# Eight heads' attention weights transposed by the DMA engines, and a written order for the last heads' steps

## The chip, the cores and the metric

The kernel runs on one core of a Trainium2 chip. The metric is the time of one execution on the device in microseconds (us), given as the median of a few runs. The engines are TensorE (PE, with its weight loads shown as PEld), VectorE (DVE), ScalarE (ACT), GpSimd (POOL) and SyncE (SP), which issues the DMAs; each works through its own queue of instructions in order and waits on semaphores for the others.

## The reference

One decoder layer on 256 tokens of width 1024, in float32. With SEQ equal to MOBA_BLOCK there is one key block, so the block selection falls away and the attention is plain causal attention with 8 heads of 128.

```python
def reference(x, attn_norm, attn_w_qkv, attn_w_o, ..., ffn_norm, ffn_w_in, ffn_w_out, final_norm):
    x = x + moba_attention(rms_norm(x, attn_norm[0]), attn_w_qkv[0], attn_w_o[0])
    x = x + swiglu(rms_norm(x, ffn_norm[0]), ffn_w_in[0], ffn_w_out[0])
    return rms_norm(x, final_norm)
# moba_attention: p = softmax(mask(q k^T / sqrt(128))); out = concat(p v) w_o
# swiglu:         g, u = split(h w_in); silu(g) * u times w_out      (hidden width 2816)
```

## The kernel before

Every large product is made as three products of parts: a float32 matrix is split into a rounded part `hi` (a cast on ACT, L84) and the rest `lo` (a subtraction on DVE, L85), and `mm` (L102 to L105) adds hi·hi, hi·lo and lo·hi in PSUM. So each weight tile of 128 x 2048 that is loaded (`early`, L99) costs two casts on ACT and two subtractions on DVE of 128 x 1024 each.

The stages follow each other: the value projection (L192), for each of 8 heads the projection of q and k (`project`), then the output projection `wo` (L335 to L340 and L354 to L372), the hidden layer of the channel mixer (`hidden`, from L389) and its output.

The attention of a head is cut into steps which lag behind each other by `follow`: `scores(h)` makes q·k on TensorE, adds the mask (DVE, L253), takes the exponential (ACT, L258) and scales by the sums (DVE, L263), which leaves the weights `pn[h]`, 128 x 384 (three 128 x 128 blocks, since the upper block of a causal mask is empty). `attend(h)` needs them transposed. It writes a PSUM bank of the pool `ps_b`, which has two, and reads it out into `oh` (ACT, L306) and `ol` (DVE, L307), the operands of head h's part of the output projection.

The transpose is done in two ways. Heads 0 to 5 (`BY_DMA = 6`): `turn_p(h)` copies the float32 weights on ACT into two planes of 16-bit halves (L269, into `planes_p`, one buffer) and has SP issue one DMA transpose of the planes (L271, into `turned_p`, two buffers); `transpose_p(h)` joins the halves again on ACT (L280). Heads 6 and 7: `transpose_p(h)` makes three transposes on TensorE (L289) into PSUM and copies the last block out on ACT (L296). Both then make `p0h` (ACT, L293) and `p0l` (DVE, L294), which `attend(h)` takes.

The output projection of a head is 12 products of 128 x 512 (`wo_mm`, two token tiles t, two halves n, three each). Before, the code goes through heads 0 to 4 and, behind each of heads 1 to 4, calls `follow`, which does the steps that are still open; heads 5 to 7 follow with the residual sums: for each (t, n) the sum is added to x (L364), multiplied by the gain (L366, `xg`), squared for the norm (ACT, L367) and transposed by four transposes on TensorE (`turn_x1`, L349), whose result is cast (ACT, L351) and subtracted (DVE, L352) as operands `x1h` and `x1l` of the hidden layer.

The code is not the order on the engines: a scheduler orders each engine's instructions from the order of the code and its own estimates, and fixes it when the program is built. A copy written within `keep_in_program_order` stays where it is written. In what follows the order is that of the built program.

## Time and profile before

| | before |
|---|---|
| median of 3 runs | 294.16 us (291.99, 294.46, 294.16) |
| the profiled execution | 292.13 us, of which span of its instructions 290.3 us |
| PE busy | 282.2 us, 97% of the span, 1481 matmuls |
| PEld busy | 241.4 us, 83% |
| DVE busy | 210.4 us, 72% |
| ACT busy | 196.8 us, 68% |
| DMA | 59.91 MB, mean 206 GB/s |
| granted TensorE clock | 0.996 of full speed |
| chain that ended last | PE 94%, DMA 2%, DVE 1%, ACT 1% |

The span goes from the first to the last instruction. Matmuls are pipelined: one is printed with 0.39 us but the next starts 0.23 us later, so what a matmul costs is read from start to start. The output projection lies at 80.8 to 107.3 us of the span.

### The profile page before, as it was taken

The page shows a single profiled execution, that of the slowest core. Times are in us where ns is not written, and L with a number is a line of the kernel's source. Part 1 is how long each engine was busy: PE and PEld are TensorE (multiplying, and loading weights), DVE is VectorE, ACT ScalarE, POOL GpSimd, SP SyncE. Part 2 cuts the span into 40 slices and gives each one's busy share as a digit, 9 for nine tenths or more (in the row PEclk, how much of TensorE's full clock was granted, in tenths as well). Part 3 has the DMA queues.
Part 4 walks back from the last instruction along what each step waited for, and adds up shares of the span by engine and source line. Part 5 has one row for each costly group of instructions (what it writes and reads, how often), then busy time and mean ns, then how long its engine had stood idle before and what let it go on. Part 6 is the DMA issues. An engine that isn't in the chain of part 4 may idle for free.

```text
span 290.3 us, 3904 instructions
## 1 busy us (share of the span) xinstructions
PE 282.2 (97%) x1481; PEld 241.4 (83%) x1481; DVE 210.4 (72%) x328; ACT 196.8 (68%) x295; POOL 1.3 (0%) x8
## 2 busy tenths in 40 slices
PE   7899999999999999999999999999999999999992
PEld 4688999999988888888888888888888888888881
DVE  3757988877776489648468468468959689987784
ACT  3786878777985388739659659659649687544443
POOL 1000000000000000000000000000000000000000
PEclk9999999999999999999999999999999999999998
DMA  6999785985565406785765875766363737770003
GB/s 202 414 424 419 284 290 102 369 264 174 172 189 218 163 38 202 256 273 164 282 215 160 277 219 159 275 212 137 144 181 54 275 54 279 281 256 35 0 0 144
DMA packets 25507, 59.91 MB, mean 206 GB/s; under 512 B 17425, under 2 KB 17809, under 8 KB 19601
## 3 DMA queue, kind: packets, MB, share of 16 engines
q1 hardware_dynamic: 25200, 59.28, 60.8%
q10 hardware_dynamic: 288, 0.39, 0.4%
q8 instruction: 11, 0.18, 0.3%
q14 instruction: 8, 0.06, 0.1%
HBM read 54.56 MB, written 1.05 MB: 192 GB/s over the span
## 4 chain that ended last, share of the span: by engine, by line
PE 94%; DMA 2%; DVE 1%; ACT 1%; SPq 0%; issue 0%
PE pmm L105 24%; PE pmm L103 24%; PE pmm L104 24%; PE pmm L192 7%; PE pb L105 2%; PE pb L104 2%; PE pb L103 2%; PE pa L104 2%; PE pa L105 2%; PE pa L103 2%; DMA first<-in_xw 2%; PE pb L349 1%; PE pb L305 1%; PE pb L247 1%; DVE x_sb L567 1%; SPq L132 0%
## 5 line engine op out<-in xcount | busy, mean ns | idle before, releaser
L85 DVE TENSOR_TENSOR lo<-raw,hi 128x1024 fp32r<-128x1024 f32 x80 | 95.9, 1221 | 22.8 <-ACT hi L84 22.7
L84 ACT CAST hi<-raw 128x1024 fp32r<-128x1024 f32 x80 | 81.5, 1048 | 12.3 <-issue 5.6
L103 PE MATMUL pmm<-hi,xh 128*128 128x512 f32 x176 | 68.6, 390 | 0.0
L104 PE MATMUL pmm<-lo,xh 128*128 128x512 f32 x176 | 68.6, 390 | 0.0
L105 PE MATMUL pmm<-hi,xl 128*128 128x512 f32 x176 | 68.5, 389 | 0.0
L105 PEld LDWEIGHTS pmm<-hi,xl 128*128 128x128 f32 x176 | 33.0, 188 | 6.9
L104 PEld LDWEIGHTS pmm<-lo,xh 128*128 128x128 f32 x176 | 33.0, 188 | 6.8
L103 PEld LDWEIGHTS pmm<-hi,xh 128*128 128x128 f32 x176 | 33.0, 188 | 6.8
L404 ACT ACTIVATE sg<-pmm,r 128x256 f32<-128x256 f32 x22 | 10.5, 476 | 30.4 <-PE pmm L105 30.4
L103 PE MATMUL pmm<-hi,first 128*128 128x512 f32 x76 | 30.2, 397 | 0.0
L104 PE MATMUL pmm<-lo,first 128*128 128x512 f32 x76 | 29.7, 390 | 0.0
L103 PE MATMUL pmm<-xh,hi 128*128 128x256 f32 x96 | 27.1, 283 | 0.0
L105 PE MATMUL pmm<-xh,lo 128*128 128x256 f32 x96 | 27.1, 283 | 0.0
L104 PE MATMUL pmm<-xl,hi 128*128 128x256 f32 x96 | 27.1, 282 | 0.0
L478 ACT CAST hi<-raw 128x1024 fp32r<-128x1024 f32 (+1 forms) x15 | 17.6, 1191 | 8.7 <-PE pa L105 3.8
L479 DVE TENSOR_TENSOR lo<-raw,hi 128x1024 fp32r<-128x1024 f32 (+1 forms) x15 | 20.5, 1397 | 3.2 <-ACT hi L478 3.2
L405 DVE SCALAR_TENSOR_TENSOR hs<-pmm,r,sg 128x256 f32<-128x256 f32 x22 | 10.5, 482 | 14.9 <-ACT sg L404 14.9
L103 PEld LDWEIGHTS pmm<-xh,hi 128*128 128x128 f32 x96 | 18.4, 192 | 0.0
L105 PEld LDWEIGHTS pmm<-xh,lo 128*128 128x128 f32 x96 | 18.4, 191 | 0.0
L104 PEld LDWEIGHTS pmm<-xl,hi 128*128 128x128 f32 x96 | 18.4, 191 | 0.0
L103 PEld LDWEIGHTS pmm<-hi,first 128*128 128x128 f32 x76 | 14.3, 188 | 2.7
L104 PEld LDWEIGHTS pmm<-lo,first 128*128 128x128 f32 x76 | 14.3, 188 | 2.7
(156 smaller groups left out, 457.6 us busy)
## 6 DMA issues: line engine op xcount, KB each, us to landing
raw<-in_w_in SPq DMA_DIRECT2D x22, 1024.0 KB, 4.9
raw<-in_w_out SPq DMA_DIRECT2D x11, 1024.0 KB, 4.8
raw<-in_wqk SPq DMA_DIRECT2D x8, 1024.0 KB, 10.8
raw<-in_wo SPq DMA_DIRECT2D x4, 1024.0 KB, 7.7
first<-in_xw SPq DMA_DIRECT2D x3, 640.0 KB, 8.1
second<-in_xw SPq DMA_DIRECT2D x2, 640.0 KB, 11.8
x_sb<-in_x SPq DMA_DIRECT2D x1, 1024.0 KB, 11.1
g_bc<-in_g SPq DMA_DIRECT2D x2, 512.0 KB, 4.5
```

The costliest lines, as they stand in the source:

```text
L84: nc.scalar.copy(hi, raw)
L85: nc.vector.tensor_sub(lo, raw, hi.bitcast(F32))
L103: nc.tensor.matmul(o, lhsT=lh, rhs=rh, start=first, stop=False)
L104: nc.tensor.matmul(o, lhsT=lh, rhs=rl, start=False, stop=False)
L105: nc.tensor.matmul(o, lhsT=ll, rhs=rh, start=False, stop=last)
L192: nc.tensor.matmul(pv[t][a // 512][:, a % 512 : a % 512 + b - a], lhsT=l[:, k, t * P : (t + 1) * P], rhs=r[:, a:b],  start=k == 0 and a % ...
L247: nc.tensor.matmul(ps[:, :P], lhsT=f[:, :P], rhs=f[:, T : T + P], start=True, stop=True)
L305: nc.tensor.matmul(po[:, P:], lhsT=v1[:, hs], rhs=p1, start=False, stop=True)
L404: nc.scalar.activation(sg, pf[t][:, 0], AF.Silu, scale=r2[t])
L405: nc.vector.scalar_tensor_tensor(hs_[c][:, :, t], pf[t][:, 1].rearrange("p (j f) -> p j f", j=2), r2[t], sg.rearrange("p (j f) -> p j f", ...
L478: nc.scalar.copy(h[:, a:b], r[:, a:b])
L479: nc.vector.tensor_sub(l[:, a:b], r[:, a:b], h[:, a:b].bitcast(F32))
```

## The change

`BY_DMA` falls away: all eight heads take the way through the planes, the DMA transpose and the join, and `transpose_p` without its TensorE branch is now `join_p`. In place of the loop with `follow` behind heads 1 to 4, the steps of heads 4 to 7 are written out between the heads' products, with parts of heads 5 and 6 moved ahead.

```diff
-        def transpose_p(h):
-            pp = joined_p[h % 2]
-            if h < BY_DMA:
...
-            else:
-                p = ps_a.tile([P, 3 * P], F32, name="pa")
-                for i in range(3):
-                    nc.tensor.transpose(p[:, i * P : (i + 1) * P], pn[h][:, i * P : (i + 1) * P], ident)
-                p1 = pp[:, T:]
...
+        def join_p(h):
+
+            p = joined_p[h % 2]
+            tc.keep_in_program_order(
+                nc.scalar.copy(
+                    p.bitcast(U16).rearrange("p (n w) -> p n w", w=2),
+                    turned_p[h % 2].rearrange("p (w n) -> p n w", w=2),
+                )
             )
             p0h = a2.tile([P, T], F32R, name="p0h")
             p0l = a2.tile([P, T], F32R, name="p0l")
             nc.scalar.copy(p0h, p[:, :T])
             nc.vector.tensor_sub(p0l, p[:, :T], p0h.bitcast(F32))
-            if h >= BY_DMA:
-                nc.scalar.copy(p1, p[:, T:])
-            pt[h] = p0h, p0l, p1
+            pt[h] = p0h, p0l, p[:, T:]
...
-                if step is scores and 0 <= i < BY_DMA:
+                if step is scores and 0 <= i < H:
                     turn_p(i)
...
-        for h in range(5):
+        def wo_head(h):
             for t in range(NT):
                 for n in range(2):
                     wo_mm(h, t, n)
-            if h:
-                follow(H + h - 1)
+
+
+        wo_head(0)
+        attend(4)
+        scores(7)
+        turn_p(7)
+        wo_head(1)
+        join_p(6)
+        attend(5)
+        wo_head(2)
+        wo_head(3)
+        join_p(7)
+        attend(6)
+        wo_head(4)
+        for h, t in ((5, 0), (6, 0)):
+            for n in range(2):
+                wo_mm(h, t, n)
+        attend(7)
+        for n in range(2):
+            wo_mm(5, 1, n)
...
-                if t == 0:
-                    for h, m in ((5, 0), (6, 0), (5, 1), (6, 1), (7, 0)) if n == 0 else ((7, 1),):
-                        wo_mm(h, t, m)
-                else:
-                    for h in range(5, H):
-                        wo_mm(h, t, n)
+                for h in (7,) if t == 0 else (6, 7):
+                    wo_mm(h, t, n)
```

What it does to the order on the engines is seen at three places. In the rows an operation is followed by what it writes, `<-`, what it reads, and the size; line numbers have shifted a little (L84 is L82 now, L280 is L277, L306 is L295, L349 is L356, L364 is L367).

On ACT, behind the exponential of head 6 (the two `third,sums` rows at the top): first before, where head 5's join (L280) and `p0h` come next,

```order
L258 ACTIVATE third,sums<-third,nm 128x128
L258 ACTIVATE third,sums<-third,nm 128x256
L280 COPY second<-second 128x768
L293 CAST p0h<-second 128x256
L84 CAST hi<-raw 128x1024
L306 CAST first<-pb 128x256
L84 CAST hi<-raw 128x1024
L293 CAST p0h<-pa 128x256
```

and now, where `first<-pb` is head 4's result, `second<-third` (L267) head 6's plane copy and `second<-second` (L277) head 5's join:

```order
L256 ACTIVATE third,sums<-third,nm 128x128
L256 ACTIVATE third,sums<-third,nm 128x256
L295 CAST first<-pb 128x256
L267 COPY second<-third 128x768
L277 COPY second<-second 128x768
L256 ACTIVATE third,sums<-third,nm 128x128
L284 CAST p0h<-second 128x256
L256 ACTIVATE third,sums<-third,nm 128x256
L82 CAST hi<-raw 128x1024
L295 CAST first<-pb 128x256
L82 CAST hi<-raw 128x1024
L267 COPY second<-third 128x768
```

Head 4's result and head 6's plane copy have moved ahead of head 5's join, and half of head 7's exponential ahead of head 5's `p0h`.

On TensorE, from head 7's last products into the hidden layer (`pmm<-hi,xh`; `pb<-ident,xg` are the four transposes of `turn_x1`). Before:

```order
L103 MATMUL pmm<-hi,first 128x512
L349 MATMUL pb<-ident,xg 128x128 x4
L104 MATMUL pmm<-lo,first 128x512
L105 MATMUL pmm<-hi,first 128x512
L349 MATMUL pb<-ident,xg 128x128 x4
L103 MATMUL pmm<-hi,first 128x512
...
L103 MATMUL pmm<-hi,xh 128x512
L349 MATMUL pb<-ident,xg 128x128 x4
L104 MATMUL pmm<-lo,xh 128x512
```

and now:

```order
L103 MATMUL pmm<-hi,first 128x512
L356 MATMUL pb<-ident,xg 128x128 x4
L101 MATMUL pmm<-hi,first 128x512
L102 MATMUL pmm<-lo,first 128x512
L103 MATMUL pmm<-hi,first 128x512
L101 MATMUL pmm<-hi,xh 128x512
L356 MATMUL pb<-ident,xg 128x128 x4
L102 MATMUL pmm<-lo,xh 128x512
```

Two groups of transposes and nine products stood between the first group and the hidden layer, now three products do; the second group stands behind the hidden layer's first product.

On DVE, the residual sums behind head 7's last subtraction (`first<-pb,first`). Before, and then now:

```order
L307 TENSOR_TENSOR first<-pb,first 128x256
L364 TENSOR_TENSOR x_sb<-pmm,x_sb 128x512 x2
L366 TENSOR_TENSOR xg<-x_sb,g_bc 128x512 x2
```

```order
L296 TENSOR_TENSOR first<-pb,first 128x256
L367 TENSOR_TENSOR x_sb<-pmm,x_sb 128x512
L83 TENSOR_TENSOR lo<-raw,hi 128x1024
L369 TENSOR_TENSOR xg<-x_sb,g_bc 128x512
L367 TENSOR_TENSOR x_sb<-pmm,x_sb 128x512
```

A subtraction of a weight tile now stands between the first sum and its `xg`. On SP the transposes of heads 6 and 7 stand behind the loads of the first four tiles of `w_in` and ahead of the fifth.

## Rows read from the trace of the kernel before

**Rows 1.** Waits of TensorE, whole span: who waited for whom, us, times, longest

```profile
PE pmm L192 <- ACT hi L84: 1.3, 3, 0.8
...
```

**Rows 2.** Windows: stretch, length, busy of PE, PEld, DVE, ACT, POOL, clock, DMA

```profile
6.00:12.00 6.00, 4.96 (x22) 3.56 (x21) 3.35 (x6) 3.69 (x7) 0.00 (x0) 1.00 1.01 398
84.00:98.00 14.00, 14.00 (x78) 11.99 (x76) 10.03 (x25) 9.18 (x21) 0.00 (x0) 1.00 0.54 195
```

**Rows 3.** Timeline of TensorE, output projection: start, us, engine, line, operation, output, input

```profile
83.58 0.39 PE L103 MATMUL pmm<-hi,first 128*128 128x512 f32 x1
...
86.30 0.28 PE L103 MATMUL pb<-p0h,first 128*128 128x256 f32 x1
...
87.46 0.49 PE L289 MATMUL pa<-ident,third 128*128 128x128 f32 x3
87.71 0.47 PE L103 MATMUL pmm<-hi,first 128*128 128x512 f32 x1
88.02 0.39 PE L104 MATMUL pmm<-lo,first 128*128 128x512 f32 x1
```

**Rows 4.** Timeline of ACT: a plane copy, joins, an exponential, a p0h

```profile
78.71 0.83 ACT L269 COPY second<-third 128x768 uint16<-128x768 uint16 x1 [0.57 <-DVE third L263]
79.45 0.92 ACT L280 COPY second<-second 128x768 uint16<-128x768 uint16 x1
...
84.06 0.41 ACT L258 ACTIVATE third<-third,nm 128x128 f32<-128x128 f32 x1 [0.67 <-DVE nm L253]
...
84.46 0.49 ACT L258 ACTIVATE third<-third,nm 128x256 f32<-128x256 f32 x1
...
84.96 0.91 ACT L280 COPY second<-second 128x768 uint16<-128x768 uint16 x1
85.90 0.41 ACT L293 CAST p0h<-second 128x256 fp32r<-128x256 f32 x1
```

**Rows 5.** Timeline of DVE in the same stretch

```profile
83.40 0.42 DVE L307 TENSOR_TENSOR first<-pb,first 128x256 fp32r<-128x256 f32 x1
...
84.29 1.22 DVE L85 TENSOR_TENSOR lo<-raw,hi 128x1024 fp32r<-128x1024 f32 x1
...
85.62 0.55 DVE L263 TENSOR_SCALAR third<-third,sums 128x128 f32<-128x128 f32 x2
```

**Rows 6.** Timeline of DVE at the residual sums, merged by twos

```profile
101.75 1.37 DVE L364 TENSOR_TENSOR x_sb<-pmm,x_sb 128x512 f32<-128x512 f32 x2 [2.61 <-PE pmm L105]
103.03 1.28 DVE L366 TENSOR_TENSOR xg<-x_sb,g_bc 128x512 f32<-128x512 f32 x2
...
105.72 0.69 DVE L366 TENSOR_TENSOR xg<-x_sb,g_bc 128x512 f32<-128x512 f32 x1
```

**Rows 7.** Timeline of TensorE at the residual sums and the hidden layer's start

```profile
103.86 0.63 PE L349 MATMUL pb<-ident,xg 128*128 128x128 f32 x4
...
107.30 0.39 PE L103 MATMUL pmm<-hi,xh 128*128 128x512 f32 x1
```

**Rows 8.** Timeline of SP: issue of the fourth w_in tile's load

```profile
85.54 0.33 SPq L99 DMA_DIRECT2D raw<-in_w_in  x1
```

**Rows 9.** The page's groups of instructions: weight casts; busy, mean ns, idle before

```profile
L84 ACT CAST hi<-raw 128x1024 fp32r<-128x1024 f32 x80 | 81.5, 1048 | 12.3 <-issue 5.6
```

**Rows 10.** The tile of planes and joins, 60 to 110 us: three DMA transposes' landing

```profile
DMA to landing us min/median/max: 2.7/4.2/4.4
```

**Rows 11.** Timeline of ACT at the residual sums and in the hidden layer

```profile
102.47 0.63 ACT L367 ACTIVATE scr<-x_sb 128x512 bf16<-128x512 f32 x1 [3.79 <-DVE x_sb L364]
...
103.15 0.63 ACT L367 ACTIVATE scr<-x_sb 128x512 bf16<-128x512 f32 x1
...
105.96 0.57 ACT L351 CAST xh<-pb 128x512 fp32r<-128x512 f32 x1
...
116.59 2.01 ACT L84 CAST hi<-raw 128x1024 fp32r<-128x1024 f32 x2 [1.62 <-PE pmm L105]
```

**Rows 12.** Line L271, 50 to 56 us: landing of head 1's DMA transpose

```profile
DMA to landing us min/median/max: 5.9/5.9/5.9
```

More of the change, by code (lines that the diff above doesn't have):

```diff
@@ L47 @@
 XK = 4
-BY_DMA = 6
 G = 64
@@ L273, in turn_p @@
             )
-        def transpose_p(h):
-            pp = joined_p[h % 2]
-            if h < BY_DMA:
-                tc.keep_in_program_order(
-                    nc.scalar.copy(
-                        pp.bitcast(U16).rearrange("p (n w) -> p n w", w=2),
-                        turned_p[h % 2].rearrange("p (w n) -> p n w", w=2),
-                    )
-                )
-                p, p1 = pp, pp[:, T:]
-            else:
-                p = ps_a.tile([P, 3 * P], F32, name="pa")
-                for i in range(3):
-                    nc.tensor.transpose(p[:, i * P : (i + 1) * P], pn[h][:, i * P : (i + 1) * P], ident)
-                p1 = pp[:, T:]
+        def join_p(h):
[4 more added lines that the diff above has]
+                    turned_p[h % 2].rearrange("p (w n) -> p n w", w=2),
+                )
+            )
             p0h = a2.tile([P, T], F32R, name="p0h")
@@ L309, in follow @@
         def follow(h):
-            for step, i in ((attend, h - 4), (scores, h - 1), (transpose_p, h - 2)):
+            for step, i in ((attend, h - 4), (scores, h - 1), (join_p, h - 2)):
                 if 0 <= i < H:
                     step(i)
-                if step is scores and 0 <= i < BY_DMA:
+                if step is scores and 0 <= i < H:
                     turn_p(i)
```

## The prediction

> **What bounds the kernel now.** I read the waits of TensorE first: after the start it waits for nothing, and its only rows are one wait of the warm-up and three, 1.3 us in all, of the value projection in the first 9 us [rows 1]. The window over the stretch of the change, 84 to 98 us, says the same the other way: 14.00 of 14.00 us busy at a granted clock of 1.00, while ACT has 9.18 and DVE 10.03 [rows 2]. So TensorE sets the end, and only two things count: what leaves or enters its queue, and every place where its next instruction now finds an input missing. I then read the timelines of the four engines at the output projection (80.8 to 107 us) for the prices and the places.
>
> **What the change removes.** The transposes of heads 6 and 7, three on TensorE each. Group one starts at 87.46 and the product behind it at 87.71, and that product takes 0.31 us to the next start where a product usually takes 0.227 (twelve of them, from 83.58 to 86.30): 0.25 + 0.08 = 0.33 us a group, 0.67 us for both [rows 3]. Nothing covers TensorE, so this is gained in full. The printed 0.49 us of a group is no price, since matmuls overlap.
>
> The Trainium skill, "VectorE: DVE Perf Modes", section "The three transpose paths", puts a 128x128 transpose (bf16) at 390 ns on TensorE and 1309 ns by DMA, and its rules ask for TensorE where PSUM will do, which speaks against this change. By that page's 390 ns the six would give back 2.3 us (an estimate), and the sum below would come to a gain of 0.3 us; the rows show less than a third of that a piece, in the stream of products, and go into the sum.
>
> **What it adds.** Per head 6 and 7 a plane copy (0.83 us) and a join (0.91 us) on ACT [rows 4] in place of one 128x128 copy out of PSUM, and one DMA transpose on SP. DVE keeps its count. ACT has 4.8 us free in that window [rows 2], so the 3.5 us are no bound as a sum; where they stand matters. On ACT and DVE the next instruction starts some 0.1 us before a printed end, so below I add start to start.
>
> **Wait 1, head 4's attend.** Before, it stands behind 24 products and starts at 86.30; now behind 12, where the thirteenth started at 83.58 [rows 3]. Its PSUM bank (pool ps_b has two) is the one of head 3's attend, which DVE's subtraction frees at 83.40 + 0.42 = 83.82 [rows 5]. From such an end to the matmul that waited is 0.14 us (the first of the two xg ends at 103.03 + 0.69 = 103.72, the transposes start at 103.86) [rows 6, 7]. It starts at 83.96: **0.38 us** lost.
>
> **Wait 2, head 5's attend.** TensorE: 83.96, then 1.16 us for attend and scores (86.30 to 87.46), then 12 + 2 products at 0.227, so it reaches head 5's at 88.30. ACT: before, head 5's join starts at 84.96 and its p0h at 85.90 [rows 4]. Now the order puts head 6's plane copy ahead of that join, and that copy needs head 6's weights. On DVE head 4's subtraction (0.34) has moved ahead of their scaling, which ends at 85.62 + 0.55 + 0.34 = 86.51 instead of 86.17 [rows 5]. Plane copy 86.55, +0.74, join 87.29, +0.82, the first half of head 7's exponential 88.11, +0.40 [rows 4], p0h 88.51 to 88.92. With 0.14 us the attend starts at 89.06: **0.76 us** lost. Queued behind it on TensorE is the rest of heads 2 and 3, which waits with it.
>
> **Heads 6 and 7 by DMA: no wait.** Head 6's transpose is issued when its planes are there, 86.55 + 0.83 = 87.4, behind the two w_in loads that SP holds ahead of it, the later of which is issued at 85.54 in both orders, since DVE's 84.29 row releases it [rows 5, 8]. ACT next: second half of the exponential 88.8, weight cast 89.3 (1.05 less the 0.1) [rows 9], head 5's result 90.3 (some 0.3, as p0h of that size), a cast, then head 7's plane copy at 91.5. The planes have one buffer, so that copy also waits for head 6's transpose: it has 91.5 - 87.4 = 4.1 us free, and 0.5 us more before TensorE, which reaches head 6's attend at 94.6 (89.06, half of the 1.16, 22 x 0.227), feels it. In this stretch a transpose lands after 2.7 to 4.4 us, median 4.2 [rows 10]; I take 4.2, as the load ahead is in flight. Cost nothing, with 0.4 us to spare. Head 7's is issued at 92.4; its join stands behind a cast that waits for head 3's last product (94.8) until 95.9, and what follows on ACT, head 6's result, is wanted by TensorE at 99.3, so up to 5 us are free. The next load of w_in now goes behind these two transposes, at about 93.6; the casts of the hidden layer's later chunks wait for a buffer that TensorE frees at 116.6 [rows 11], so that is covered.
>
> **Wait 3, the start of the hidden layer.** Before, two groups of x1 transposes stand among head 6's and 7's products, and the cast of the first starts at 105.96, 1.3 us ahead of the first hidden product at 107.30 [rows 7, 11]. Now tile 0's sums end later and its first transposes stand three products before the hidden layer. TensorE reaches head 7's products at 102.6 (99.3, 6 products, head 7's attend, 6 products) and ends the first block's three at 103.45, their last by the printed 0.39. DVE adds it at 103.5 (0.64), then in the new order a weight subtraction (1.22 less 0.1), then xg from 105.3 to 106.0 [rows 5, 6]; with 0.14 us the transposes start at 106.1, **0.1 us** after TensorE is there. DVE's next add (0,1) ends at 106.6; ACT has the square of that add in its queue ahead of the cast: 106.65 + 0.68, cast 107.35 + 0.57 = 107.9 [rows 6, 11], the product at 108.05. TensorE comes to it at 106.1 + 0.44 (four thirds of 0.33) + 0.68 = 107.25: **0.80 us** lost. That weight subtraction is the larger part of the cause.
>
> **Sum.** 0.38 + 0.76 + 0.10 + 0.80 = 2.04 us of waits, less 0.67 us: **+1.37 us**. Against the profiled execution's own 292.13 us (span 290.3 and 1.8 around it) that is 293.5. The four executions shown fall in two pairs, 291.99 and 292.13, 294.16 and 294.46; the median, 294.16, is 2.0 above the profiled one. I forecast on the median: 294.16 + 1.37 = **295.5 us**. Its own range is 0.1 us more or less at each of the four waits and half of the last one either way, 0.8 in all: +0.6 to +2.2, or 294.7 to 296.3.
>
> **Rivals.**
> *The waits don't come*, since ACT or DVE run ahead there by half a microsecond more than the order gives. For it: TensorE waited nowhere in the old order, and the largest wait is under 0.8 us. Against: each is a chain of rows with the end on one instruction. It gives -0.67 us, 293.5 us. The point: p0h of head 5 ready by 88.2.
> *The DMA lands late*, the one that ends slower. With two wo loads in flight one transpose took 5.9 us [rows 12]; here one load is in flight. Up to 4.6 us costs nothing; past it head 6's attend is late one for one, and head 7's join, which holds head 6's result, once more. At 5.9 us that is 5.9 - 4.6 = 1.3 and 5.9 - 5.0 = 0.9, so +2.2 us, in all +3.6 or 297.7 us. From about 5.5 us on it is over 1% slower.
> *The clock falls* in a wait, to the 1.2 GHz level, and each microsecond of products there takes two. Against: TensorE waited 1.3 us in pieces up to 0.8 at the start, and the granted clock stood at 1.00 behind it too [rows 1, 2]. Three microseconds of it would give +4.4, 298.5 us.
> That the change isn't made can be excluded: no row of the new order has a transpose of these weights on TensorE.
>
> **Chances.** Forecast 0.70, no waits 0.15, late DMA 0.10 (0.06 of it past 5.5 us), clock 0.03, 0.02 for a gain that I don't see. 1% is about what a measurement of this kernel can tell from no change, some 2.9 us. No case but the last reaches that as a gain: faster 0.02. Slower: 0.03 of the forecast, if its waits are twice as long, 0.06 and 0.03: 0.12. Within 1%: 0.86. The range must hold either pair of executions: from the lower pair (292.06) with most of the transposes' gain kept, 291.8, to the upper (294.3) with late landings of some 5.4 us, 297.1.
>
> **What would show it.** In the changed trace: no transposes of these weights on TensorE, waits of TensorE on DVE at head 4's attend (0.4), on ACT's p0h at head 5's (0.8), on ACT's cast xh at the first hidden product (0.8), and none at heads 6 and 7 with landings under 4.6 us. TensorE busy over 84 to 98 us falls from 14.00 to about 13. It would be wrong if TensorE shows no wait (then 293.5), if p0l of head 6 is late (a landing over 4.6), or if the first hidden product starts before 107.5 or after 109 us.

## The result, and the profile after

| | before | after |
|---|---|---|
| median of 20 runs each, side by side | 292.45 us (291.73 to 294.46) | 293.62 us (292.73 to 296.57) |
| ratio after to before | | 1.0054, 95% interval 1.0033 to 1.0076 |
| the profiled execution | 292.13 us, span 290.3 | 295.51 us, span 293.7 |
| PE busy | 282.2 us, 1481 matmuls | 282.6 us, 1475 matmuls |
| ACT busy | 196.8 us | 199.4 us |
| granted TensorE clock | 0.996 | 0.995 |

The change makes the kernel slower by 0.54%, 1.6 us (1.0 to 2.2 by the interval). The two medians differ by 1.2 us. The forecast was +1.37 us.

The waits of TensorE in the profile after: who waited for whom, us, times, longest. They answer to [rows 1].

```profile
PE pmm L190 <- ACT hi L82: 1.7, 3, 1.1
PE pb L142 <- DVE eps L138: 1.2, 1, 1.2
PE pb L101 <- DVE first L296: 1.1, 1, 1.1
PE pmm L101 <- DVE qk L233: 0.6, 1, 0.6
PE pmm L101 <- ACT xh L358: 0.4, 1, 0.4
PE pb L101 <- ACT p0h L284: 0.2, 1, 0.2
```

The first two stood in the kernel before too (the value projection and the warm-up). Of the four new ones three were forecast: head 4's attend for DVE, head 5's for ACT's `p0h`, the first hidden product for ACT's `xh`. The fourth, for `qk`, is the tenth product of the output projection, the first that goes into the last of its four PSUM banks, from which DVE had not yet read head 7's `qk`; it was not forecast.

The window 84 to 98 us, the columns as in [rows 2]:

```profile
84.00:98.00 14.00, 12.70 (x63) 10.29 (x64) 9.36 (x25) 11.06 (x23) 0.00 (x0) 1.00 0.62 188
```

TensorE is busy for 12.70 us where it was for all 14.00, at the same clock, and ACT has 11.06 us of work for 9.18.

The timeline of TensorE after, at the four places, each with the product ahead of it:

```profile
83.03 0.39 PE L103 MATMUL pmm<-hi,first 128*128 128x512 f32 x1
83.98 0.50 PE L101 MATMUL pmm<-hi,first 128*128 128x512 f32 x1 [0.56 <-DVE qk L233]
...
84.54 0.40 PE L103 MATMUL pmm<-hi,first 128*128 128x512 f32 x1
86.02 0.35 PE L101 MATMUL pb<-p0h,first 128*128 128x256 f32 x1 [1.07 <-DVE first L296]
...
90.24 0.39 PE L102 MATMUL pmm<-lo,first 128*128 128x512 f32 x1
90.85 0.39 PE L101 MATMUL pb<-p0h,first 128*128 128x256 f32 x1 [0.23 <-ACT p0h L284]
...
108.98 0.40 PE L103 MATMUL pmm<-hi,first 128*128 128x512 f32 x1
109.79 0.50 PE L101 MATMUL pmm<-hi,xh 128*128 128x512 f32 x1 [0.41 <-ACT xh L358]
```

A wait is read here from start to start. The bracket counts only from the modelled end of the product ahead, 0.39 us behind its start, but in the stream the next product starts 0.23 us behind it. So the step less 0.23 is what is lost: 0.72 at 83.98, 1.25 at 86.02, 0.38 at 90.85, 0.58 at 109.79. "Lost" is used in this sense below, also where the bracket is missing because the gap is short.

ACT after: head 6's exponential, its plane copy, head 5's join and `p0h`, and, for the hidden layer, the square of the second residual sum (`scr`) and the cast behind it. They answer to [rows 4] and [rows 11].

```profile
86.11 0.40 ACT L256 ACTIVATE third<-third,nm 128x128 f32<-128x128 f32 x1 [0.67 <-DVE nm L251]
...
88.44 0.83 ACT L267 COPY second<-third 128x768 uint16<-128x768 uint16 x1 [1.09 <-DVE third L261]
89.18 0.92 ACT L277 COPY second<-second 128x768 uint16<-128x768 uint16 x1
...
90.41 0.39 ACT L284 CAST p0h<-second 128x256 fp32r<-128x256 f32 x1
...
108.54 0.63 ACT L370 ACTIVATE scr<-x_sb 128x512 bf16<-128x512 f32 x1 [1.13 <-DVE x_sb L367]
...
109.17 0.56 ACT L358 CAST xh<-pb 128x512 fp32r<-128x512 f32 x1
```

The order is the forecast one: the plane copy ahead of the join, the join 0.74 us behind it, `p0h` 1.23 us behind the join. But the whole row of instructions stands later than before: the exponential at 86.11, where it was at 84.06 [rows 4]. TensorE itself is only 0.36 us later there (head 3's attend starts at 80.01, before at 79.65).

DVE after: the subtraction that frees the bank for head 4's attend, and the weight subtraction ahead of the gain product (`xg`) at the residual sums:

```profile
85.45 0.41 DVE L296 TENSOR_TENSOR first<-pb,first 128x256 fp32r<-128x256 f32 x1
...
106.09 1.22 DVE L83 TENSOR_TENSOR lo<-raw,hi 128x1024 fp32r<-128x1024 f32 x1
107.22 0.68 DVE L369 TENSOR_TENSOR xg<-x_sb,g_bc 128x512 f32<-128x512 f32 x1
```

The line of the DMA transposes after: from issue to landing, of head 1's (issued at 52.2), head 6's (89.3) and head 7's (94.5), one row each:

```profile
DMA to landing us min/median/max: 7.6/7.6/7.6
...
DMA to landing us min/median/max: 4.2/4.2/4.2
...
DMA to landing us min/median/max: 2.7/2.7/2.7
```

Heads 6 and 7 land within the 4.6 us that the forecast allowed, and their attends show no wait. Head 1's took 7.6 us where it took 5.9 before [rows 12]; the section on what was not expected comes back to it.

### The profile page after: what moved, and what is told of

Read it like the earlier page. It is cut to its first block, busy times and chain, and to the rows that moved or that the text cites. A ratio compares the mean times of both kernels' runs of the same rounds, so it can differ in the third digit from the quotient of the medians.

```text
span 293.7 us, 3902 instructions
## 1 busy us (share of the span) xinstructions
PE 282.6 (96%) x1475; PEld 240.4 (82%) x1475; DVE 209.8 (71%) x328; ACT 199.4 (68%) x297; POOL 1.3 (0%) x8
## 3 DMA queue, kind: packets, MB, share of 16 engines
HBM read 54.56 MB, written 1.05 MB: 189 GB/s over the span
## 4 chain that ended last, share of the span: by engine, by line
PE 77%; DVE 9%; ACT 5%; DMA 5%; issue 2%; SPq 0%; DVEq 0%; ACTq 0%
PE pmm L103 19%; PE pmm L101 19%; PE pmm L102 19%; PE pmm L190 7%; DVE lo L83 4%; DMA second<-second 3%; PE pa L102 2%; PE pa L103 2%; PE pa L101 2%; DMA first<-in_xw 2%; PE pb L101 2%; PE pb L103 2%; PE pb L102 2%; ACT second L277 2%; ACT hi L82 1%
## 5 line engine op out<-in xcount | busy, mean ns | idle before, releaser
L82 ACT CAST hi<-raw 128x1024 fp32r<-128x1024 f32 x80 | 81.6, 1048 | 13.9 <-PE pmm L103 8.3
```

Of the source, the lines that this page charges most:

```text
L82: nc.scalar.copy(hi, raw)
```

## The experiments

My theory was that the written order costs, by three waits that together are more than the 0.67 us that the six TensorE transposes give back. Rival A: the DMA way of heads 6 and 7 costs by itself. Rival B: the difference is only the late landing of head 1's transpose in the profiled execution. Runs of one batch share the runs of the kernel before on the same chip.

The table has what each profile lost and, in the last two columns, the stretch from the first product of head 3's attend to the last product of the program (79.65 to 284.38 before, 204.73 us) as a difference to that, and the timed ratio. This stretch leaves out the load stage and the store of the result, which differ from execution to execution. "Lag" is the start of head 6's exponential on ACT behind the first product of head 3's attend on TensorE (84.06 - 79.65 = 4.41 before).

| kernel | lag | head 4's attend | head 5's | head 6's | head 7's | first hidden | stretch | ratio to before (95%) |
|---|---|---|---|---|---|---|---|---|
| before | 4.41 | 0 | 0 | 0 | 0 | 0 | 204.73 | |
| after | 6.10 | 1.25 (and 0.72 ahead) | 0.38 | 0 | 0 | 0.58 | +2.72 | 1.0054 (1.0033 to 1.0076) |
| after, again | 5.40 | 1.25 | 0.42 | 0 | 0 | 0.58 | +2.06 | 1.0046 (1.0025 to 1.0066) |
| all by DMA, old order | 4.35 | 0 | 0 | 1.03 | 0 | 0 | +0.77 | 1.0032 (1.0017 to 1.0048) |
| new order alone | 4.33 | 0.31 | 0 | 0 | 0 | 0.58 | +1.14 | 1.0034 (1.0016 to 1.0051) |
| tile 0 first | 4.29 | 0.26 | 0.40 | 0 | 0 | 0 | +0.22 | 1.0015 (1.0003 to 1.0027) |
| head 5's join first | 4.33 | 0.31 | 0 | 0.58 | 0 | 0.58 | +1.49 | 1.0079 (1.0059 to 1.0099) |
| other bank | 5.17 | 0 | 1.05 | 0 | 0 | 0.65 | +1.82 | 1.0041 (1.0024 to 1.0058) |
| three undone | 4.69 | 0 | 0 | 1.65 | 0 | 0 | +3.04 | 1.0079 (1.0052 to 1.0105) |
| old order, later attends | 4.40 | 0 | 0 | 0 | 0 | 0 | +0.35 | 1.0027 (1.0009 to 1.0046) |
| head 6's join first | 4.26 | 0 | 0 | 0 | 1.00 | 0 | +0.68 | 1.0031 (1.0013 to 1.0049) |
| head 6's attend later | 5.06 | 0 | 0 | 0 | 1.21 | 0 | +0.98 | 1.0034 (1.0017 to 1.0050) |
| before, doubled transpose | 4.95 | 0 | 0 | 0 | 0 | 0 | +0.28 | 1.0015 (0.9998 to 1.0031) |
| after, doubled transpose | 4.79 | 0.67 | 0 | 0 | 0 | 0.58 | +1.07 | 1.0057 (1.0034 to 1.0081) |

Three gaps stand in none of these columns: in "other bank" and in "head 6's attend later" head 7's scores lose 0.47 and 0.26 us, and in "head 5's join first" and "three undone" the second matmul of head 6's attend comes another 0.3 to 0.4 us late. The parts don't add up to the stretch exactly: the doubled transpose in the kernel before brings +0.28 us with no gap that stands out, so up to 0.3 us of this column can come without one.

### The two halves of the change

```diff
-BY_DMA = 6
+BY_DMA = 8
```

> Heads 6 and 7 transposed by the DMA engines as in the changed kernel, but the order of the steps around them is left as before: one edit alone. Theory (the new order costs, not the way of the transpose): the six TensorE transposes go, which is worth 0.67 us by the two groups of [rows 3], and one wait comes, of head 6's attend for ACT's joined copy, about 1.3 us, since in the old order that step stands only 8 to 9 us behind head 6's plane copy: +0.5 to +0.9 us against the kernel before (ratio 1.002 to 1.003). The order of the hidden layer's start is the old one, so no wait of 0.4 us or more there. Rival A (the DMA way itself costs the +1.5 us that the change cost): this kernel is slower by +1.2 us or more, with the wait on the landing of the two transposes.

Measured 1.0032, +0.9 us. The timeline of TensorE in this kernel, at head 6's attend:

```profile
93.56 0.39 PE L104 MATMUL pmm<-lo,first 128*128 128x512 f32 x1
94.82 0.39 PE L103 MATMUL pb<-p0h,first 128*128 128x256 f32 x1 [0.87 <-ACT p0h L293]
```

It is the one wait that was expected, 1.03 us lost where about 1.3 was forecast, and the time is at the upper end of what the theory gave (rival A's +1.2 us lies inside the interval of the measurement, 0.5 to 1.4 us). The landing itself was in time: issued at 86.78, it took 4.1 us, so it was there at 90.9, while ACT waited for head 7's weights from DVE, copied their planes at 92.68 and did head 6's join only at 93.42, behind them. So neither theory is the whole of it. The landing costs nothing here, as the theory had it, but the ACT work that comes with the DMA way does, in an order that isn't made for it: rival A isn't refuted, it is the copies and not the landing by which it holds here.

The other half, TensorE's transposes of heads 6 and 7 in the new order (core of the edit):

```diff
-        for h in range(5):
+        wo_head(0)
+        attend(4)
+        scores(7)
+        wo_head(1)
+        transpose_p(6)
+        attend(5)
...
-                    for h, m in ((5, 0), (6, 0), (5, 1), (6, 1), (7, 0)) if n == 0 else ((7, 1),):
-                        wo_mm(h, t, m)
+                for h in (7,) if t == 0 else (6, 7):
+                    wo_mm(h, t, n)
```

> The other half alone: heads 6 and 7 are still turned by TensorE, but the steps of the last heads stand in the written order of the change and the rest of the output projection ends as in it. Theory: the gain of 0.67 us isn't there, the wait of head 4's attend for its PSUM bank comes (0.4 to 1.1 us), head 5's attend finds its copy in time, as TensorE's join of head 6 puts no plane copy ahead of head 5's join on ACT, and the hidden layer's start waits as in the changed kernel (0.4 to 0.8 us): +0.8 to +1.5 us against the kernel before (ratio 1.003 to 1.005). Rival A (the DMA way costs): within 0.4 us of the kernel before.

Measured 1.0034, +1.0 us, within the theory's range and outside rival A's 0.4. Its timeline of TensorE at the hidden layer's start:

```profile
106.51 0.40 PE L105 MATMUL pmm<-hi,first 128*128 128x512 f32 x1
107.32 0.51 PE L103 MATMUL pmm<-hi,xh 128*128 128x512 f32 x1 [0.41 <-ACT xh L368]
```

The same step, 0.81 us, as in the profile after. The bank's wait is 0.31 us, and head 5's attend loses nothing, since here no plane copy of head 6 stands ahead of head 5's join. So the order costs without the DMA way, and the wait at head 5 needs both.

### One wait taken away at a time

The tail: head 7's attend stands ahead of head 6's products, and tile 1's products of heads 5 to 7 come last, as cover.

```diff
-        for h, t in ((5, 0), (6, 0)):
-            for n in range(2):
-                wo_mm(h, t, n)
+        for n in range(2):
+            wo_mm(5, 0, n)
         attend(7)
         for n in range(2):
-            wo_mm(5, 1, n)
+            wo_mm(6, 0, n)
...
-                for h in (7,) if t == 0 else (6, 7):
+                for h in (7,) if t == 0 else (5, 6, 7):
```

> The changed kernel, but of the output projection's last products those of tile 0 are done first: head 7's attend stands before head 6's products, and the products of heads 5, 6 and 7 for tile 1 stand last, as cover of the hidden layer's norm. Theory: the wait of the first hidden product for ACT's cast (0.41 us in the profile of after, 0.80 by the forecast) is gone and the load stage's start is early again: 0.5 to 0.9 us less than the changed kernel, so +0.6 to +1.0 us against the kernel before (ratio 1.002 to 1.0035). Rival A and rival B, which put the cost ahead of 98 us: same as the changed kernel, +1.5 us.

Measured 1.0015, +0.4 us (0.1 to 0.8): better than the expected +0.6 to +1.0. The timeline of TensorE at the three places:

```profile
83.01 0.39 PE L103 MATMUL pmm<-hi,first 128*128 128x512 f32 x1
83.50 0.35 PE L101 MATMUL pb<-p0h,first 128*128 128x256 f32 x1
...
87.70 0.39 PE L102 MATMUL pmm<-lo,first 128*128 128x512 f32 x1
88.33 0.38 PE L101 MATMUL pb<-p0h,first 128*128 128x256 f32 x1 [0.24 <-ACT p0h L284]
...
106.92 0.39 PE L103 MATMUL pmm<-hi,first 128*128 128x512 f32 x1
107.15 0.39 PE L101 MATMUL pmm<-hi,xh 128*128 128x512 f32 x1
```

The first hidden product follows at the stream's own 0.23 us. The first pair shows the bank's wait at its natural size, 0.49 - 0.23 = 0.26 us, too short to be printed as one. The tail is the largest part of the price, and it lies behind 98 us, where neither rival puts it.

Head 5's join ahead of head 6's plane copy:

```diff
-            for step, i in ((attend, h - 4), (scores, h - 1), (join_p, h - 2)):
+            last = ((scores, h - 1), (turn_p, h - 1), (join_p, h - 2))
+            if h == H - 1:
+                last = ((scores, h - 1), (join_p, h - 2), (turn_p, h - 1))
+            for step, i in ((attend, h - 4), *last):
...
-                if step is scores and 0 <= i < H:
-                    turn_p(i)
```

> The changed kernel with one line's order changed: at the step of head 7, head 5's join (ACT) stands ahead of head 6's plane copy and DMA transpose. Theory: head 5's attend no longer waits for ACT (0.2 us in the profile of after, 0.76 us by the forecast); what is saved is 0.2 to 0.5 us against the changed kernel, so +1.0 to +1.3 us against the kernel before (ratio 1.0035 to 1.0045), since the bank's wait and the hidden layer's start stay. Rival A (the landing of the DMA transposes costs): head 6's transpose is issued about 0.7 us later, so the step would become slower by as much, +2.2 us. Rival B (all of the difference is a late landing of head 1's transpose near 58 us, which the edit doesn't touch): same as the changed kernel, +1.5 us.

Measured 1.0079, +2.3 us over six runs: the theory missed, rival A's number is the one that came. Head 5's attend loses nothing any more, but head 6's does, 0.58 us. TensorE, then ACT, in this kernel:

```profile
93.12 0.39 PE L103 MATMUL pmm<-hi,first 128*128 128x512 f32 x1
93.93 0.39 PE L101 MATMUL pb<-p0h,first 128*128 128x256 f32 x1 [0.42 <-ACT p0h L284]
...
91.78 0.83 ACT L267 COPY second<-third 128x768 uint16<-128x768 uint16 x1 [2.02 <-DMA second<-second]
92.52 0.93 ACT L277 COPY second<-second 128x768 uint16<-128x768 uint16 x1
```

ACT sits idle for 2.02 us until head 6's transpose has landed, then copies head 7's planes, which have the same single buffer, and only then joins head 6. The transpose was issued at 86.56 and took 5.1 us, where it took 4.0 to 4.2 in after, in all by DMA and in tile 0 first, which leave the join where it was. The profiled execution (293.40) has the lowest time of the six, so the others lost more, but no profile of one of those shows where.

The PSUM bank:

```diff
-            po = ps_b.tile([P, T], F32, name="pb")
+            po = ps_a.tile([P, T], F32, name="pa") if h >= 4 else ps_b.tile([P, T], F32, name="pb")
```

> The changed kernel, but the attends of heads 4 to 7 write another PSUM bank (of ps_a, unused by then), so that head 4's attend need not wait for VectorE to have read head 3's. Theory: that wait goes, and head 5's attend, which stands 13 products behind, waits longer by the same amount, as its copy on ACT comes no earlier: within 0.3 us of the changed kernel, +0.8 to +1.3 us against the kernel before. Rival: each wait costs for itself, so 0.3 to 0.4 us less than the changed kernel.

Measured 1.0041, against 1.0046 of the unchanged after in the same batch: no difference that can be told. TensorE in this kernel:

```profile
84.48 0.38 PE L245 MATMUL pb<-qk 128*128 128x128 f32 x1 [0.31 <-DVE first L296]
...
88.14 0.39 PE L102 MATMUL pmm<-lo,first 128*128 128x512 f32 x1
89.41 0.39 PE L101 MATMUL pa<-p0h,first 128*128 128x256 f32 x1 [0.89 <-ACT p0h L284]
```

Head 4's attend goes through, head 7's scores now wait for the bank instead, and head 5's attend loses 1.05 us where it lost 0.42. So the profile has it as the theory did, and a wait that is taken away only moves to the next one behind it as long as the operand there comes at the same time; the times alone can't tell this from the rival's 0.3 to 0.4 us.

### The changed kernel once more

> The changed kernel as it is, once more, to have a profile in which head 1's DMA transpose lands as early as in the kernel before. In the profile of after that transpose finished 7.6 us after its issue (5.9 us before), and ScalarE and VectorE ran 2.05 us later from 58 us on. Theory (the three waits of the written order make the difference, and the late landing only decides which of them is long): with the early landing the wait of head 4's attend is small (0.3 us or less, a longer step between two products), head 5's attend waits 0.3 to 0.8 us, the first hidden product 0.4 us or more; +0.9 to +1.3 us against the kernel before (ratio 1.003 to 1.0045). Rival B (the difference is the late landing): no more than +0.4 us when it lands early.

Measured 1.0046, +1.3 us; the edge of the theory's range. The early landing that was to be had didn't come: it took 6.9 us, and ACT's lag is 5.40. So this run didn't test rival B as meant. TensorE and ACT:

```profile
83.47 0.39 PE L103 MATMUL pmm<-hi,first 128*128 128x512 f32 x1
84.95 0.36 PE L101 MATMUL pb<-p0h,first 128*128 128x256 f32 x1 [1.09 <-DVE first L296]
...
85.04 0.41 ACT L256 ACTIVATE third<-third,nm 128x128 f32<-128x128 f32 x1 [0.67 <-DVE nm L251]
```

It did show that head 4's attend loses 1.25 us with this lag, where it lost 0.26 to 0.31 with a lag of 4.3.

### Lateness on purpose

```diff
-            nc.sync.dma_start_transpose(
...
+            for _ in range(2 if h == 1 else 1):
+                nc.sync.dma_start_transpose(
...
```

In the kernel before:

> The kernel before, with head 1's DMA transpose issued twice, one after the other (its result is the same): this makes its landing later on purpose, by some 3 to 5 us. Theory (a late landing of that transpose puts ACT and VectorE behind for the rest of the attention, in either kernel): the kernel before then pays 1.5 to 4 us, its attends waiting for ACT in the load of the output projection. Rival: ACT has the slack to make it up, so less than 0.5 us.

And in the kernel after:

> The same with the changed kernel: head 1's DMA transpose issued twice. Theory (late landing is common to both kernels, and the order's waits come on top): 1.0 to 1.6 us slower than the kernel before with the same doubling. Rival B (the difference between the two kernels is nothing but the late landing): equal to it within 0.4 us.

Measured 1.0015 and 1.0057. The kernel before pays +0.4 us (-0.1 to +0.9), as its rival had it, and the theory's 1.5 to 4 us did not come: no attend waits. The changed kernel is 1.0057 - 1.0015 = 0.42%, 1.2 us, slower than it, as expected; the two medians differ by 1.1 us, and rival B's 0.4 us is at the edge of what the spread of the runs allows. Head 4's attend in the changed kernel (TensorE), then the copy of head 2's planes in the kernel before with the doubled transpose (ACT), which needs the buffer that the doubled transpose reads:

```profile
82.83 0.39 PE L103 MATMUL pmm<-hi,first 128*128 128x512 f32 x1
83.73 0.39 PE L101 MATMUL pb<-p0h,first 128*128 128x256 f32 x1 [0.51 <-DVE first L297]
...
62.15 0.83 ACT L269 COPY second<-third 128x768 uint16<-128x768 uint16 x1 [0.83 <-DMA second<-second]
```

The edit did not make ACT late by what it was meant to. The second of the two transposes lands at 62.1 (61.8 in the changed kernel), some 4 us later than the single one of before (57.7), and the plane copy starts at 62.15 where it started at 57.84. But the built order is another: two weight casts, a `qkh` and an attend's result now stand ahead of that copy, and the lag at head 6's exponential is 4.95 and 4.79, only 0.54 and 0.38 us more than before. What lags of 5.4 or 6.1 cost the kernel before is therefore not shown.

The changed kernel lost 0.67 us at a lag of 4.79. With the others: 0.26 to 0.31 at 4.29 to 4.33, 0.67 at 4.79, 1.25 at 5.40, and 1.25 + 0.72 at 6.10. The loss grows by about as much as the lag does. In the old order the same attend stands twelve products, 2.7 us, later, and in no profile of that order, the largest lag of which is 4.95, did it lose anything.

### Four tries to keep the gain

With all three waits undone (other bank from head 3 on, head 5's join first, tile 0 first), and head 5's attend one group of products later:

```diff
         wo_head(0)
-        attend(4)
         scores(7)
+        attend(4)
         turn_p(7)
         wo_head(1)
         join_p(6)
-        attend(5)
         wo_head(2)
+        attend(5)
         wo_head(3)
```

> The changed kernel with all three waits taken away at once: the attends of heads 3 to 7 write the other PSUM bank; head 7's scores stand before head 4's attend and head 5's attend one product group later, with head 5's join ahead of head 6's plane copy; and the last products of tile 0 are done first, as in the run with that edit alone. Theory: the gain of 0.67 us is left, less about 0.4 us at head 6's attend, whose transpose is now issued later: -0.4 to 0.0 us against the kernel before if head 6's transpose lands within 4.8 us of its issue, up to +0.4 us if it takes 5.4 us. Rival A (the DMA way of heads 6 and 7 costs by itself): +0.7 us or more.

Measured 1.0079, +2.3 us: the theory missed, and the number is one that rival A allows. The three waits are gone, and one at head 6's attend has come, for a transpose that landed after 5.1 us. TensorE there:

```profile
93.16 0.39 PE L103 MATMUL pmm<-hi,first 128*128 128x512 f32 x1
95.04 0.38 PE L101 MATMUL pa<-p0h,first 128*128 128x256 f32 x1 [1.49 <-ACT p0h L284]
...
96.71 0.63 PE L102 MATMUL pmm<-lo,first 128*128 128x512 f32 x1
97.14 0.63 PE L103 MATMUL pmm<-hi,first 128*128 128x512 f32 x1
```

And the window behind it:

```profile
96.00:98.80 2.80, 2.80 (x9) 2.27 (x8) 2.46 (x3) 2.25 (x4) 0.00 (x0) 0.50 0.41 82
```

The step of 1.88 us between two products is the longest in the fourteen profiles from head 3's attend on. The granted clock was still 1.00 when the products began again (95.0 to 95.6), then stood at 0.50, the 1.2 GHz level, for some 3.4 us (95.9 to 99.3), and the products followed each other by 0.43 us; until that wait, from 83 to 93 us, TensorE had been busy throughout at 1.00. In the column of the stretch (+3.04) this is about 1.4 us: the seven steps from 96.14 to 99.27 took 3.13 us, in the stream they take some 1.70.

The old order, with the attends of heads 6 and 7 later:

```diff
-BY_DMA = 6
+BY_DMA = 8
...
-            if h:
+            if 0 < h < 3:
                 follow(H + h - 1)
+            if h == 4:
+                follow(H + 2)
+        for n in range(2):
+            wo_mm(5, 0, n)
+        for n in range(2):
+            wo_mm(6, 0, n)
+        follow(H + 3)
...
-                    for h, m in ((5, 0), (6, 0), (5, 1), (6, 1), (7, 0)) if n == 0 else ((7, 1),):
+                    for h, m in ((7, 0),) if n == 0 else ((7, 1),):
```

> The old order with all heads transposed by DMA (the first experiment), and only the steps of heads 6 and 7 moved: head 6's attend stands behind the products of head 4 and head 7's behind those of heads 5 and 6 for tile 0. Theory: the wait of 0.9 us at head 6's attend is gone and the 0.67 us show, less 0.3 to 0.5 us for a first product that waits for VectorE and for a hidden layer that starts with less cover: -0.3 to +0.3 us against the kernel before. Rival A (the DMA way costs): as the first experiment or slower, +0.9 us.

Measured 1.0027 (1.0009 to 1.0046), +0.8 us: the theory's band reached +0.3, so it missed by half a microsecond, and rival A's 0.9 is the nearer. Its profile has no wait of an attend, and its stretch is 0.35 us above that of before, inside what the theory gave and less than the timed ratio says. Several short steps too long, 0.1 to 0.2 us each, stand in it (at 98.0, 98.3, 99.4 and 107.1). The profiled execution (292.31 us) is 0.7 us faster than the kernel's median; where the rest of the timed difference lies is open.

Then two other ways of undoing all three waits, of which the diffs show only the order of the steps; first head 6's join ahead of head 7's planes, with the old place of head 5's join:

```diff
-        attend(4)
         scores(7)
-        turn_p(7)
+        attend(4)
         wo_head(1)
         join_p(6)
-        attend(5)
+        turn_p(7)
         wo_head(2)
+        attend(5)
         wo_head(3)
+        attend(6)
         join_p(7)
-        attend(6)
```

> All three waits of the changed kernel taken away, as in the run with three undone, but by other moves: the attends of heads 3 to 7 write the other PSUM bank; head 7's scores stand before head 4's attend; head 5's attend stands behind the products of head 2 (no change to head 5's join); and head 6's join on ACT stands ahead of head 7's plane copy, since in the profiles the join of head 6 waited behind that copy (0.74 us), and the copy itself behind the landing of head 6's transpose, which reads the same buffer. The last products of tile 0 are done first. Theory (the three waits are the whole price of the change): the 0.67 us of the six transposes are left over, -0.7 to -0.3 us against the kernel before (ratio 0.9975 to 0.999). Rival A (the DMA way of heads 6 and 7 costs by itself): +0.5 us or more.

Measured 1.0031, +0.9 us: the theory missed, and rival A's number came. Nothing is lost at heads 4, 5 and 6 and at the hidden layer, and 1.00 us at head 7. SyncE's issues, ACT and TensorE:

```profile
92.41 0.33 SPq L97 DMA_DIRECT2D raw<-in_w_in  x1
93.36 1.21 SPq L269 DMA_TRANSPOSE second<-second  x1
...
98.43 0.92 ACT L277 COPY second<-second 128x768 uint16<-128x768 uint16 x1 [1.97 <-DMA second<-second]
...
98.61 0.39 PE L103 MATMUL pmm<-hi,first 128*128 128x512 f32 x1
99.84 0.38 PE L101 MATMUL pa<-p0h,first 128*128 128x256 f32 x1 [0.84 <-ACT p0h L284]
```

Head 7's transpose is now issued behind a weight load of 1 MB and takes 5.0 us; in the profile after it is issued ahead of that load and takes 2.7. ACT waits 1.97 us for it.

Second, head 5's join first, head 6's attend behind head 4's products, and, beyond what the expectation names, head 7's plane copy behind head 1's products:

```diff
         wo_head(0)
+        scores(7)
         attend(4)
-        scores(7)
+        wo_head(1)
         turn_p(7)
-        wo_head(1)
         join_p(6)
+        wo_head(2)
         attend(5)
-        wo_head(2)
         wo_head(3)
         join_p(7)
+        wo_head(4)
         attend(6)
-        wo_head(4)
...
```

> As the run with three undone (other PSUM bank, head 5's join ahead of head 6's plane copy, tile 0's products first), but head 6's attend stands behind the products of head 4, so that a landing of head 6's transpose 5.1 us after its issue, which cost 1.5 us of wait and then the clock in that run, is still in time. Theory: no wait between 80 and 107 us, the clock stays, -0.7 to -0.3 us against the kernel before. If head 6's transpose lands later than that: the wait of head 6's attend is back and the time is +1 us or more.

Measured 1.0034, +1.0 us. Head 6's transpose took 5.7 us and was in time for its attend, as meant, but head 7's planes could be copied only when it had landed, and head 7's attend lost 1.21 us. That is the second case of the expectation, at another head.

No arrangement that was run is faster than the kernel before. The nearest, tile 0 first, is slower by 0.15% (0.03 to 0.27%). So the written order costs without the DMA way (new order alone, +1.0 us), and the DMA way costs in the old order (+0.9 us) and in four orders made to avoid the waits: my theory names the waits of the changed kernel, but rival A, that the DMA way of heads 6 and 7 costs something of its own, stands beside it. What tile 0 first would take with those heads transposed on TensorE was not run. Rival B falls: the profile of the new order alone has the early landing (5.8 us) and is longer by 1.14 us.

## Why the prediction was right, and where it was not

**The difference**: forecast +1.37 us, measured +1.57 us in the first comparison (0.54%) and +1.34 us in the second (0.46%). **The time**, 293.62 us, lies in the range of the prediction (291.8 to 297.1) but 1.9 us below the forecast 295.5 us and below that forecast's own range, which began at 294.7. The step that failed there is the base: it was put on the median of three runs, 294.16, while twenty runs have 292.45, 1.7 us less. Put on the profiled execution, the prediction's other base, the sum was 293.5. That the profiled execution after happens to have 295.51 us is no support: it is the one with a landing of 7.6 us.

**The gain**, 0.67 us: not contradicted, and never seen alone. In the run with tile 0 first the sum of the parts is -0.67 + 0.26 + 0.40 = 0.0, and 0.11 us more where a product of the output projection stands between the matmuls of head 5's attend and makes a step of 0.22 us instead of 0.11 (the product's own 0.23 is no loss); the stretch says +0.22. What is left over is 0.1 us, but as the stretch of the doubled kernel before is 0.28 us longer without a wait, the 0.67 us are not confirmed closer than by some 0.3. The Trainium skill, "VectorE: DVE Perf Modes", section "Rules for kernel authors", asks for a 128x128 transpose on TensorE where PSUM will do, by which the change should lose; every kernel here with heads 6 and 7 by DMA was slower than before, from 1.0015 to 1.0079, which agrees with the rule. But the 390 ns against 1309 ns (for bf16) that the Trainium skill gives on the same page, section "The three transpose paths", are not the reason that the traces show: the six cost 0.11 us each in the stream, and the DMA way is dear by its landing of 2.7 to 5.7 us and by the ACT copies on both sides of it.

**Wait 1**, head 4's attend for its bank: forecast 0.38; 0.26 to 0.31 in the three profiles whose lag is that of before, so the mechanism and size are right there. What failed is that the step took ACT's and DVE's times from one execution as if they were fixed: at the larger lags it is 0.67 to 1.97 us.

**Wait 2**, head 5's attend for `p0h`: forecast 0.76, measured 0.38 to 0.42. The order on ACT is as forecast, and from the plane copy to `p0h` it took 88.44 to 90.41, 1.97 us, as forecast (86.55 to 88.51). The size was off by three small parts. TensorE came 0.1 us later than forecast: the attend started 4.83 us behind head 4's (86.02 to 90.85), of which it lost 0.38 to 0.40, so it was there after 4.43 to 4.45, forecast 88.30 - 83.96 = 4.34. The plane copy stood 2.42 us behind head 4's attend (88.44), forecast 86.55 - 83.96 = 2.59. And the attend started 0.05 us behind `p0h`'s printed end (90.41 + 0.39), where I had taken 0.14. Together 0.36 us. The run with the new order alone, which has no plane copy there, loses nothing, so the named cause stands.

**Heads 6 and 7 by DMA**: no wait forecast, none there; landings 4.2 and 2.7 us for 4.2 taken. The limit of 4.6 us in that step was not put to the test in the changed kernel; that 5.1 us at head 6 brought a wait in two kernels with another order fits it.

**Wait 3**, the hidden layer's start: forecast 0.10 + 0.80. The first hidden product lost 0.58 us; the whole of the tail is had by the difference of after, again and tile 0 first, 2.06 - 0.22 = 1.84 us of stretch, of which head 4's and head 5's attends take (1.25 + 0.42) - (0.26 + 0.40) = 1.01: 0.83 us. The cause that was named, a weight subtraction ahead of `xg` on DVE and the square ahead of the cast on ACT, is in the rows (106.09 and 107.22; 108.54 and 109.17). The run with tile 0 first takes both away at once, so how much belongs to the subtraction, which the prediction called the larger part, is not shown.

**The sum**, at the lag of before, is by these -0.67 + 0.3 + 0.4 + 0.83 = +0.9 us instead of +1.37; the lag adds 1.0 us at 5.40 and 1.7 us at 6.10. The measured +1.3 to +1.6 lies between; what lag the timed runs had is not on record. So the forecast difference is right partly by luck, by misses that cancel: waits 2 and 3 a little too dear, and a wait 1 that is cheap on paper and varies.

**The rivals**: late landings of heads 6 and 7 did not come in the changed kernel but did in four arrangements with other orders (5.0 to 5.7 us), and so did the fall of the clock in one of them, for which I gave 0.03; the ground given against it, that waits up to 0.8 us left the clock at 1.00, said nothing about a longer one. TensorE busy over 84 to 98 us was to fall to about 13: it is 12.70. The first hidden product was to start between 107.5 and 109 us: it does at 108.73 in after, again, but at 109.79 in after. By the prediction's own sign that profile is outside: TensorE had lost 1.97 us up to head 4's attend, where the sum had 0.38 and no term for a late landing of head 1's transpose.

## What to carry over

An early step in an engine that never waits is not priced by where its operands stand in one profile: a step moved twelve products ahead lost by about as much as the other engines' lag grew (0.3 us at 4.3, 1.25 at 5.4). In the old place it lost nothing at lags up to 4.95; that the 2.7 us of products ahead of it there would cover larger ones is an estimate. A short operation taken off the bounding engine (0.67 us here) was outweighed by what replaced it on the others, and taking one wait away moved it to the next place where the operand came no earlier. And of the edits to the changed kernel, doing tile 0's last products first, with the other tile's as cover for its norm and transposes, is the one that helped: 0.8 us of the stretch, and a timed ratio of 1.0015 where the changed kernel had 1.0046 or more.

## What the runs showed of the hardware that was not expected

**A landing at 58 us can set ACT's place at 85 us.** Head 1's DMA transpose is issued behind two loads of 1 MB of the output projection's weights. Over the profiles with one transpose per head, from issue to landing and lag:

| landing of head 1's transpose | lag of ACT at head 6's exponential |
|---|---|
| 5.8 to 5.9 us (seven profiles, before among them) | 4.26 to 4.41 us |
| 6.2 | 4.69 |
| 6.6 | 5.06 |
| 6.7 | 5.17 |
| 6.9 | 5.40 |
| 7.6 | 6.10 |

One for one, four heads later: ACT takes its instructions in the built order and copies the next planes only when the transpose has landed (59.89 in after, idle for 3.32 us before it), and with this order the lag is not made up. It isn't a law: in the two kernels with the doubled transpose, whose order differs, a landing some 4 us later left a lag only 0.4 to 0.5 us larger. Whether the highest of the timed runs (up to 296.57 us) are those with a late landing is open; it fits that the two profiled executions of after with 6.9 and 7.6 us are 294.47 and 295.51 us, above their kernel's medians.

**A DMA transpose of the same size lands after 2.7 to 7.6 us**, by what is ahead of it on SP's queue. At heads 6 and 7 it was 2.7 or 2.8 when the load issued ahead had landed before, and 3.5 to 5.7 when one of 1 MB was in flight. In all sixteen cases of the second kind it landed 0.6 to 0.8 us behind that load. So three of the four late ones (twice 5.1, and 5.7) stand behind loads that took 6.2 to 6.9 us themselves, where the others took 4.9 to 5.3, and the fourth (5.0) was issued only 0.95 us behind its load; why those three loads were slow is open. Head 1's transpose too landed 0.6 to 0.8 us behind the second of its two loads, except in after, where it was 2.3 us.

**The clock**: steps of up to 1.48 us between two products left the granted clock at 1.00; the one of 1.88 us was followed, some 0.8 us after the products had begun again, by about 3.4 us at 0.50.
